# V of the second pass in seven products, and the scaling of head outputs one step later

## The chip, the cores and the metric

The kernel runs on one core of a Trainium2 chip. The metric is the device time of one execution in microseconds (us). Four engines do the work: TensorE (PE) multiplies, VectorE (DVE) and ScalarE (ACT) work elementwise, GpSimd (POOL) does some small operations; SyncE (SP) issues all transfers, on one queue.

## What is computed

One layer over 2048 tokens of width 1024. The core of the reference:

```python
h = rms_norm(x, g_pre[l]) * (1.0 + scale) + shift
(pv, pg, hq, hf, hi, hg, mg_pool, mg_hgrn) = jnp.split(h @ w_in[l], split_idx, axis=-1)
...
v = hi.astype(jnp.float32).reshape(shp)
o = hgrn2(q, k, v, logf)
o = rms_norm(o, hgrn_norm_g[l]).astype(x.dtype).reshape(b, s, HGRN_WIDTH)
branch_b = (o * jax.nn.silu(hg)) @ w_hgrn_o[l]
merged = jax.nn.sigmoid(mg_pool) * branch_a + jax.nn.sigmoid(mg_hgrn) * branch_b
y = merged @ w_out[l]
x = x + gate * rms_norm(y, g_post[l])
```

`hgrn2` is a gated linear recurrence over 8 heads of width 128, taken in chunks; branch A is a mixer of running means. V is `hi`: h times 1024 columns of `w_in`.

## The kernel before

The tokens go through in two passes of 1024, each as two halves `t` of 512 tokens. Numbers are split into a high and a low float32r part (`split`, L171: ACT casts the high part, DVE subtracts for the low part), and each product is taken as three matmuls (high x high, high x low, low x high), all with 512 columns moving.

A pass has these stages. **V** (`v_job`, L760): tokens on the stationary side, so V comes out with tokens on partitions; for each half `t`, each 512 columns `grp` and each k of 8 there are 4 token tiles x 3 matmuls, into four banks of the pool `pj`. ACT copies the four tiles (L787) and they are stored to DRAM (`Vd`), from where each head loads its part (`v_head`). **Heads** (loop at L1040): for each head three `quad`s (L469): fq (f and q), m (the two merge gates), gp (pool part and gate). A quad computes a 2 x 2 block product with the two token halves as columns, in seven products of 4 x 3 matmuls each instead of eight (Winograd's form of Strassen's scheme). The seven forms of h it needs (B11, B21, B22, T1 to T4) stay in SBUF in high and low parts: 7 x 4 x 2 = 56 of the 76 shared tiles of 128 x 512 (`up`, `utile`). **a_job, b_job**: the two branch projections. **y_job**: the last product, the norm and the residual.

The forms of h come from `h_in` (L436: four transposes on PE, then ACT, then the split) and `h_mix` (L456: four DVE differences, then four splits; "mix" below). In the second pass h of the second half and the four mixes are made during V: `x_cols` and `h_in` after each `v_job`, the mixes during the jobs of `t == 1` (L1026 to L1037).

Inside the head loop the recurrence of each head runs as two generators `hgrn` (L522, one per token half), of which every `tick()` (L961) does one step. There are six ticks in a quad and three more per head, 21 in all. The step of interest is near the end of `hgrn`, L679 to L698, and falls into the m quad of the next head (in head 7: its gp quad): after the output matmuls `po`, ACT sums squares (`junk`, L687), POOL takes the power -0.5 (`ss`, L688 and L689), ACT scales `on` (L692), and three steps later PE transposes it (`pot`, L698). In `quad`, the copy of bank `a` into bank `d` (L496: `pdfq`, `pdm`, `pdgp`) comes after the product T3, and product T4 is accumulated onto it.

Weights: `take()` (L266) gives the next item and prepares up to LOOK = 4 items ahead. In the first pass an item is loaded raw (`raw_load`, L174, buffers `wr`), combined and split into `whl` (buffers `whl`, four), and items that come again are stored to DRAM scratch (`keep`, L187); in the second pass they are loaded from there (`again`, L192). The order of the work on each engine follows the order in the code, except that an instruction whose inputs are late may be put behind others when the program is built.

Of the kernel before, what the change touches and what calls it, by code (L numbers as in the profile page):

```python
# [33 lines left out]
MASK_W = P + 2 * 64 + 5 * NT * 64  # L34
NU = 76
GAP = 5
KINDS = (("m", "gp"), ("gp", "m"))


# [30 lines left out]
def tile_block(ctx: ExitStack, tc: tile.TileContext, x, c, w_ada, b_ada, g_pre, g_post, w_in,  # L70
# [20 lines left out]
    def utile(name, dt=F32):  # L91
        return up.tile([P, T], dt, tag="u", name=name)
# [115 lines left out]
    def quad_items(key, oa, ob, keep_it):  # L208
# [37 lines left out]
            return [f0, f1, f2, f3, lambda: one(4, "21"), lambda: one(5, "12"), lambda: one(6, "22")]  # L246
        items.append((7, make))

    early = {}
    pending = []  # L250

# [41 lines left out]


    psa = [ph.tile([P, T], F32, tag=f"ph{i}", name=f"psa{i}") for i in range(2)]
    shv = cst.tile([P, 8], F32, name="shv")
    scv = cst.tile([P, 8], F32, name="scv")

# [223 lines left out]
    def hgrn(p, h, t, cx):  # L522
# [270 lines left out]
        cx["V"][h] = vt  # L793


    def two_out(nm, p, i, t, src, cx, stay):
# [42 lines left out]
    def b_job(p, j, cx):  # L839
        ps = [bank(f"psB{p}_{j}_{t}") for t in range(2)]  # L840
        sm = sig_in(p, j, 1, cx)
        for half in range(2):
            w = take()
            for t in range(2):
                three(ps[t], w, [cx["gG"][4 * half + i, t] for i in range(4)], half == 0, half == 1)
        for t in range(2):
            a, b = cx["a"].pop((j, t)), sm[t]
            tt(b, ps[t], b)
            tt(a, a, b, op=ADD)
            hi, lo = utile(f"mgh{p}_{j}_{t}", F32R), utile(f"mgl{p}_{j}_{t}", F32R)  # L850
            split(a, hi, lo)
            cx["mg"][j, t] = (hi, lo)
# [9 lines left out]
    def y_job(p, t, nn, q, cx):  # L862
# [36 lines left out]
        for tk in range(NT):  # L899
# [5 lines left out]
            for n2 in (0, 1):  # L905
# [9 lines left out]
                else:  # L915
                    outs.append(o)


    cxs = []
    for p in range(NPASS):  # L920
        cx = {k: {} for k in ("sm", "F", "Q", "G", "V", "pw", "Gd", "Pd", "Sd", "gP", "gG", "a", "mg", "x", "xc", "h32",
                              "mv", "y", "yss")}
        cx["Vd"] = dram(f"Vd{p}", [P, 8, D])
        for h in range(NH):
            cx["Gd"][h] = dram(f"Gd{p}_{h}", [P, 2, 2, T])
        for g in range(NG):
            cx["Pd"][g] = dram(f"Pd{p}_{g}", [P, 2, 2, T])
        for j in range(KT):
            for w in range(2):
                cx["Sd"][j, w] = dram(f"Sd{p}_{j}_{w}", [P, 2, T])  # L930
        cxs.append(cx)

    def krow(src, k, o):
        return src[k * P:(k + 1) * P, o:o + T]

    for p in range(NPASS):
# [17 lines left out]
        for t in range(2):  # L954
# [50 lines left out]
    for p in range(NPASS):  # L1005
        cx = cxs[p]

        mixes = [lambda p=p, i=i, cx=cx: h_mix(p, i, cx) for i in range(4)]
        if p == 0:
            head_in(0)  # L1010
            for q in range(4):
                hook = None
                if q < 3:
                    hook = lambda q=q: head_in(q + 1)
                if q == 3:
                    xss = [x_rows(NT + tk, SP.dma_start) for tk in range(NT)]
# [6 lines left out]
        vj = [(t, grp, q) for t in range(2) for grp in range(2) for q in range(4)]  # L1023
# [12 lines left out]
        while mixes:  # L1036
            once(mixes)  # L1037

        v_head(p, 0, cx)
        for h in range(NH):  # L1040
            if h + 1 < NH:
                v_head(p, h + 1, cx)
            n = f"{p}_{h}"

            def fq(row, t, u):
                (f_got, q_got)[row](p, h, t, u, cx)

            def gp(row, t, u):
                if row == 1:
                    g_got(p, h, t, u, cx)  # L1050
                elif h % 2 == 1:
                    pg_got(p, h // 2, t, u, cx)
                else:
                    gen = pv_got(p, h // 2, t, u, cx)
                    next(gen)
                    active.append(gen)

            steps = []

            def tick_in():  # L1060
                tick()
                once(steps)

            quad("fq" + n, cx, fq, tick)
            active.extend(hgrn(p, h, t, cx) for t in range(2))
            tick()
            for i, kind in enumerate(KINDS[h == NH - 1]):
                if kind == "gp":
                    quad("gp" + n, cx, gp, tick)
# [5 lines left out]
                tick()  # L1075
            if p + 1 < NPASS:
                x_stats(8 + h)

        for j in range(KT):
# [22 lines left out]
        for t in range(2):  # L1102
# [32 lines left out]
```

## Time and profile before

| | us |
|---|---|
| median of 3 runs | 1851.86 (1851.43 to 1857.75) |
| profiled execution | 1851.48 |
| its span, first to last instruction | 1849.7 |
| TensorE busy in the span | 1782.6 (96%) |
| VectorE / ScalarE busy | 1089.1 / 799.9 |

The span is what the profile shows; some 1.8 us of the execution lie around it. Matmuls are pipelined, so a busy TensorE is not at its peak, and the ends of matmuls are modelled. An engine's idle time counts only where it makes TensorE wait.

### The profile page before, as it was taken

To read this page: it belongs to the slowest core of one execution; us is meant where nothing else is said; L and a number is where in the kernel's file an instruction comes from. 1 tells how busy PE (TensorE), PEld (TensorE's weight loads), DVE (VectorE), ACT (ScalarE), POOL (GpSimd) and SP (SyncE) were. 2 spreads that over 40 slices of the span, in tenths; PEclk is the share of its full clock that TensorE was granted. 3 is DMA by queue.
4 is the path that set the end of the run, shared out by engine and by line. 5 is a ranking of instruction groups with operands and counts; after the bars stand their busy time and mean duration, and the time that the engine had idled before them with its cause. 6 is when DMAs were issued, how large, how long until landed. Compare 5 with 4: busy or idle time off the path is not lost.

```text
span 1849.7 us, 31713 instructions
## 1 busy us (share of the span) xinstructions
PE 1782.6 (96%) x12053; PEld 1456.7 (79%) x12053; DVE 1089.1 (59%) x2328; ACT 799.9 (43%) x1863; POOL 80.0 (4%) x136
## 2 busy tenths in 40 slices
PE   5999999999999999999999999999999999999997
PEld 4788878878888777787788778878888788788886
DVE  7568877887888884565432255465455456533322
ACT  4746656656556562223322335445344344311111
POOL 1100000000000000000000000000000000000000
PEclk9999999999999999999999999999999999999999
DMA  8697676676767759987887765664764764694476
GB/s 298 233 322 277 221 268 243 231 261 225 266 241 246 247 201 320 361 288 255 295 310 242 246 193 175 224 206 154 234 205 159 231 201 162 233 340 163 141 258 230
DMA packets 236530, 444.19 MB, mean 240 GB/s; under 512 B 18989, under 2 KB 109786, under 8 KB 236378
## 3 DMA queue, kind: packets, MB, share of 16 engines
q1 hardware_dynamic: 236378, 442.17, 69.9%
q8 instruction: 95, 1.56, 0.3%
q14 instruction: 57, 0.47, 0.1%
HBM read 269.61 MB, written 172.49 MB: 239 GB/s over the span
## 4 chain that ended last, share of the span: by engine, by line
PE 79%; ACT 6%; DMA 3%; DVE 3%; POOL 2%; issue 2%; SPq 1%; POOLq 0%; DVEq 0%; ACTq 0%
PE psB L278 9%; PE psV L278 8%; PE psy L278 8%; PE pafq L278 6%; PE pagp L278 6%; PE pam L278 5%; PE pefq L278 5%; PE psA L278 4%; PE pegp L278 4%; PE pem L278 3%; PE psa L278 3%; PE pbfq L278 2%; PE pbm L278 2%; PE pdfq L278 2%; PE pdm L278 2%; PE pbgp L278 2%
## 5 line engine op out<-in xcount | busy, mean ns | idle before, releaser
L172 DVE TENSOR_TENSOR whl<-wr,whl 128x512 fp32r<-128x512 f32 x210 | 143.7, 689 | 83.6 <-ACT whl L172 82.6
L172 ACT CAST whl<-wr 128x512 fp32r<-128x512 f32 x210 | 129.8, 620 | 128.6 <-DMA wr<-in_w_hgrn_o_dram 22.4
L278 PE MATMUL psy<-whl,mgh 128*128 128x512 f32 x512 | 160.1, 393 | 1.4 <-DVE y L390 0.7
L278 PE MATMUL psV<-whl,hB 128*128 128x512 f32 x512 | 161.3, 397 | 0.1
L278 PE MATMUL psB<-Gh,whl 128*128 128x512 f32 x512 | 158.6, 390 | 0.0
L578 DVE COPY_PREDICATED PT<-mask,psa 128x256 f32<-128x256 uint8 x160 | 86.1, 548 | 51.5 <-PE psa L278 51.5
L278 PEld LDWEIGHTS psy<-whl,mgh 128*128 128x128 f32 x512 | 95.0, 188 | 22.5 <-DMA whl<-scr_y 1.7
L278 PEld LDWEIGHTS psB<-Gh,whl 128*128 128x128 f32 x512 | 96.1, 188 | 20.5 <-issue 0.5
L278 PEld LDWEIGHTS psV<-whl,hB 128*128 128x128 f32 x512 | 96.6, 191 | 19.8 <-ACT V L787 0.3
L278 PE MATMUL psV<-whl,lB 128*128 128x512 f32 x256 | 100.8, 395 | 0.0
L278 PE MATMUL psB<-Gl,whl 128*128 128x512 f32 x256 | 100.0, 391 | 0.0
L278 PE MATMUL psy<-whl,mgl 128*128 128x512 f32 x256 | 100.0, 391 | 0.0
L278 PE MATMUL pam<-hT,whl 128*128 128x512 f32 x256 | 87.2, 402 | 0.0
L278 PE MATMUL pagp<-hT,whl 128*128 128x512 f32 x256 | 86.1, 397 | 0.0
L278 PE MATMUL psA<-Ph,whl 128*128 128x512 f32 x256 | 82.6, 397 | 3.4 <-DVE sm L390 1.7
L278 PE MATMUL pafq<-hT,whl 128*128 128x512 f32 x256 | 84.0, 389 | 0.0
L390 DVE TENSOR_TENSOR K<-K,TT 128x256 f32<-128x256 f32 x192 | 81.2, 424 | 1.0 <-PE psa L278 0.9
L278 PEld LDWEIGHTS psa<-X,K 128*32 128x32 f32 x2816 | 50.1, 110 | 29.8 <-issue 21.1
L172 ACT CAST mgh<-sm 128x512 fp32r<-128x512 f32 x32 | 19.7, 620 | 121.3 <-DVE sm L390 121.3
L390 DVE TENSOR_TENSOR y<-psy,gg 128x512 f32<-128x512 f32 x32 | 21.9, 688 | 73.9 <-ACT jy L893 73.7
L278 PE MATMUL psa<-X,K 128*32 128x48 f32 (+2 forms) x2816 | 61.0, 208 | 2.1 <-DVE PT L572 2.1
L572 DVE COPY_PREDICATED PT<-mask,psa 128x256 f32<-128x256 uint8 (+1 forms) x96 | 51.9, 541 | 18.3 <-PE psa L278 18.3
(358 smaller groups left out, 4307.5 us busy)
## 6 DMA issues: line engine op xcount, KB each, us to landing
wr<-in_w_in_dram SPq DMA_DIRECT2D x122, 256.0 KB, 4.4
whl<-scr_y SPq DMA_DIRECT2D x48, 512.0 KB, 4.4
sm<-Sd SPq DMA_DIRECT2D x64, 256.0 KB, 4.3
whl<-scr_v SPq DMA_DIRECT2D x32, 512.0 KB, 3.4
wa<-in_w_ada_dram SPq DMA_DIRECT2D x32, 256.0 KB, 5.4
x<-in_x_dram SPq DMA_DIRECT2D x32, 256.0 KB, 5.5
Vd<-V SPq DMA_DIRECT2D x32, 256.0 KB, 2.4
scr_v<-whl SPq DMA_DIRECT2D x16, 512.0 KB, 2.8
```

Source lines behind the costliest of these rows:

```text
L172: return A.copy(hi, src32), V.tensor_tensor(lo, src32, hi.bitcast(F32), op=SUB)
L278: PE.matmul(o, lhsT=l, rhs=r, start=start, stop=stop, skip_group_check=True)
L390: return (e or V).tensor_tensor(o, a, b, op=op)
L572: V.copy_predicated(dst.rearrange("p (c a) b -> p c a b", c=NT), m.unsqueeze(1).broadcast_to(shp), src.unsqueeze(2).broadcast_to(shp))
L578: V.copy_predicated(dst.rearrange("p (c q) a b -> p c q a b", c=NT), m, src.rearrange("p c (a b) -> p c a b", b=b).unsqueeze(2) .broadcast ...
```

## The change

Two switches are added, `FAST_V, FAST_Y = True, False`; what `FAST_Y` guards (the same form for y) is not executed, and is left out below.

1. In `hgrn`, one of the three `yield`s after the scaling moves ahead of it, so that `on` is issued one tick later; `pot` stays in its tick.
2. V of the second pass is taken by `rows7`, in seven products over both token halves and both column halves at once. The tokens' forms B11, B21, T1, T2, T3, B22, T4 are the stationary side; the moving side are seven combinations ("factors") of V's weights, 4 items each. B11, T2, T3, T4 accumulate in the four banks of `pj`, the products B21, T1 and B22 go to four other banks (`side`: the two of the scores and the two of `px`).
3. The factors are made in the first pass by `row_factors`, in 56 steps taken at every second tick of the head loop, in half widths of 256 columns, and stored to DRAM; the first pass's V weights are not stored any more.
4. The calls of `h_in` and the mixes that lay beside V are issued from `v_step`: h during B11, the mixes during B21.
5. The two score banks get new tiles at the head loop of each pass.

```diff
+    def row_factors(key, src):
+        steps = []
+        W = T // 2
+        for i in range(4):
+            for c0 in (0, W):
+                r = {}
+                def put(f, nm, i=i, c0=c0, r=r):
+                    w = utile(f"rf{key}{f}{i}{c0}", F32R)
+                    hi, lo = w[:, 0:W], w[:, W:T]
+                    split(r[nm], hi, lo)
...
+                    store((key, f, i), scr[key, f, i].rearrange("p (z n) -> p z n", z=2)[:, :, c0:c0 + W],
+                          w.bitcast(F32).rearrange("p (z n) -> p z n", z=2))
+                def ld(i=i, c0=c0, r=r):
+                    a, b = utile(f"ra{key}{i}{c0}"), utile(f"rb{key}{i}{c0}")
+                    for w, k in ((a, 2 * i), (b, 2 * i + 1)):
+                        SP.dma_start(...)
...
+                steps += [ld, nop, lambda two=two: two((0, "11"), (1, "12")),
+                          lambda two=two, a=sums: two(a, (2, "s1")),
+                          lambda two=two, a=sums2: two(a, (3, "11")),
+                          lambda two=two, a=sums3: two((4, "21"), a),
+                          lambda two=two: two((5, "12"), (6, "22"))]
+        return steps
...
         tt(ss, ss, mh[:, 0:NT], op=ALU.pow, e=G)
+        yield
         on = utile("on" + n)
         for cc in range(NT):
             A.activation(on[:, cc * P:(cc + 1) * P], po[:, cc, :], AF.Copy, scale=ss[:, cc:cc + 1])
-        yield
         yield
         yield
...
+    def rows7(name, mv, got, step):
+        acc = [bank(f"ra{name}{tk}") for tk in range(NT)]
+        c, s, u = ([utile(f"r{z}{name}{tk}") for tk in range(NT)] for z in "csu")
+        def done(nm, tk, ps):
+            if nm == "B11":
+                A.copy(c[tk], ps)
+            elif nm == "B21":
+                tt(c[tk], ps, c[tk], op=ADD)
+                got(0, 0, tk, c[tk])
+            elif nm == "T1":
+                A.copy(s[tk], ps)
...
+            else:
+                got(1, 0, tk, ps)
+        for nm in ("B11", "B21", "T1", "T2", "T3", "B22", "T4"):
+            ps = acc
+            if nm in ("B21", "T1", "B22"):
+                ps = [side(f"rx{name}{nm}{tk}", tk) for tk in range(NT)]
...
+            for i in range(2):
+                w = take()
+                for tk in range(NT):
+                    mul(i, w, tk)
+                step(nm, i)
+            ws = [take(), take(LOOK - 1)]
+            for tk in range(NT):
+                for i in (2, 3):
+                    mul(i, ws[i - 2], tk)
+                done(nm, tk, ps[tk])
+            step(nm, 2)
...
     for p in range(NPASS):
-        for t in range(2):
+        if p > 0 and FAST_V:
+            factor_items("v7")
+        for t in range(0 if p > 0 and FAST_V else 2):
             for grp in range(2):
                 for k in range(KT):
-                    plain_item(("v", grp, k), krow(w_in, k, O_I + grp * T), None, t == 1)
+                    plain_item(("v", grp, k), krow(w_in, k, O_I + grp * T), None, t == 1 and not FAST_V)
...
+            def v_step(nm, i):
+                if nm == "B11":
+                    for _ in range(len(late) if i == 2 else 2):
+                        once(late)
+                elif nm == "B21":
+                    for _ in range(2 if i == 2 else 1):
+                        once(mixes)
+            rows7(f"V{p}", cx["mv"], v_got, v_step)
...
+        psa[:] = [ph.tile([P, T], F32, tag=f"ph{i}", name=f"psa{p}_{i}") for i in range(2)]
+        behind_heads = []
+        if p == 0 and FAST_V:
+            behind_heads += row_factors("v7", w_in[:, O_I:O_I + D])
...
+        def htick():
+            tick()
+            every[0] += 1
+            if every[0] % 2 == 0:
+                once(behind_heads)
```

In the head loop `htick` takes the place of `tick`.

## Rows read from the trace of the kernel before

**Rows 1.** The page, part 1: busy us (share of the span) and instructions.

```profile
PE 1782.6 (96%) x12053; PEld 1456.7 (79%) x12053; DVE 1089.1 (59%) x2328; ACT 799.9 (43%) x1863; POOL 80.0 (4%) x136
```

**Rows 2.** Waits of PE: line, waited for; us in total, times, longest.

```profile
PE pdm L278 <- ACT pdm L496: 14.4, 12, 1.3
...
PE pdgp L278 <- ACT pdgp L496: 3.2, 2, 2.1
```

**Rows 3.** Timeline of ACT in head 1, first pass: start, us, line, operation.

```profile
234.06 1.14 ACT L692 ACTIVATE on<-po,ss 128x128 f32<-128x128 f32 x4 [1.41 <-POOL ss L390]
235.07 0.29 ACT L687 ACTIVATE junk<-po 128x128 bf16<-128x128 f32 x1
...
238.20 1.14 ACT L692 ACTIVATE on<-po,ss 128x128 f32<-128x128 f32 x4 [1.62 <-POOL ss L390]
239.22 0.61 ACT L496 COPY pdm<-pam 128x512 f32<-128x512 f32 x1
```

**Rows 4.** Timeline of POOL, the same head: the power of the second token half.

```profile
236.98 1.19 POOL L390 TENSOR_TENSOR ss<-ss,mh 128x4 f32<-128x4 f32 x1
```

**Rows 5.** Timeline of PE, the same head, from product T3 of m to gp.

```profile
235.54 0.39 PE L278 MATMUL pam<-hT,whl 128*128 128x512 f32 x1
...
238.26 0.39 PE L278 MATMUL pem<-hB,whl 128*128 128x512 f32 x1
239.89 0.50 PE L278 MATMUL pdm<-hT,whl 128*128 128x512 f32 x1 [1.24 <-ACT pdm L496]
...
242.75 1.04 PE L698 MATMUL pot<-ident,on 128*128 128x128 f32 x8
...
246.66 0.50 PE L278 MATMUL pegp<-hT,whl 128*128 128x512 f32 x1
```

**Rows 6.** Chain that ended last, through the second pass's V: start, us, what.

```profile
949.70 5.50 PE psV L278 x24
...
972.51 0.44 PE xT L444 x4
972.94 65.34 PE psV L278 x288
```

**Rows 7.** Timeline of DVE: one weight's low part, then the second pass's V.

```profile
240.48 0.68 DVE L172 TENSOR_TENSOR whl<-wr67s,whl 128x512 fp32r<-128x512 f32 x1
...
952.31 4.06 DVE L911 SCALAR_TENSOR_TENSOR xr<-y,yss,xr 128x512 f32<-128x512 f32 x6 [0.51 <-POOL yss L390]
...
974.50 0.69 DVE L172 TENSOR_TENSOR lB<-h,hB 128x512 fp32r<-128x512 f32 x1 [5.29 <-ACT hB L172]
975.11 0.68 DVE L390 TENSOR_TENSOR t<-h,h 128x512 f32<-128x512 f32 x1
...
998.36 0.69 DVE L390 TENSOR_TENSOR t<-h,h 128x512 f32<-128x512 f32 x1
...
1003.60 0.68 DVE L390 TENSOR_TENSOR t<-h,h 128x512 f32<-128x512 f32 x1
```

**Rows 8.** Timeline of PE early in the run.

```profile
39.47 1.05 PE L332 MATMUL psa<-one,acc 128*128 128x1 f32 x8 [1.37 <-DVE acc L325]
...
42.01 0.63 PE L278 MATMUL psV<-whl,hB 128*128 128x512 f32 x1
42.43 0.63 PE L278 MATMUL psV<-whl,lB 128*128 128x512 f32 x1
```

**Rows 9.** Busy us by stretch: PE, PEld, DVE, ACT, POOL, PEclk, DMA share, GB/s.

```profile
40.00:45.00 5.00, 5.00 (x20) 4.00 (x19) 4.01 (x10) 3.38 (x6) 0.00 (x0) 0.66 0.46 136
...
80.00:132.00 52.00, 52.00 (x235) 43.18 (x234) 34.89 (x56) 29.33 (x51) 0.00 (x0) 1.00 0.90 315
...
203.00:276.00 73.00, 70.78 (x575) 58.06 (x574) 58.55 (x129) 43.51 (x106) 3.89 (x6) 1.00 0.72 249
```

**Rows 10.** Groups by line and shape: a DVE operation on 128x256; busy, mean ns.

```profile
L390 DVE TENSOR_TENSOR K<-K,TT 128x256 f32<-128x256 f32 x192 | 81.2, 424 | 1.0 <-PE psa L278 0.9
```

**Rows 11.** DMA issues: transfers, KB each, median us to landing.

```profile
wr<-in_w_in_dram SPq DMA_DIRECT2D x122, 256.0 KB, 4.4
```

More of the change, by code (lines that the diff above doesn't have):

```diff
@@ L295, in tile_block, with side @@
     psa = [ph.tile([P, T], F32, tag=f"ph{i}", name=f"psa{i}") for i in range(2)]
+    def side(name, i):
+        if i < 2:
+            return ph.tile([P, T], F32, tag=f"ph{i}", name=name)
+        return px.tile([P, T], F32, tag="px", name=name)
     shv = cst.tile([P, 8], F32, name="shv")
@@ L793, in v_head, with mul @@
         cx["V"][h] = vt
+    def rows7(name, mv, got, step):
[9 more added lines that the diff above has]
+                A.copy(s[tk], ps)
+            elif nm == "T2":
+                tt(u[tk], ps, s[tk], op=ADD)
+            elif nm == "T3":
+                tt(s[tk], ps, s[tk], op=ADD)
+                got(1, 1, tk, s[tk])
+            elif nm == "B22":
+                tt(u[tk], ps, u[tk], op=ADD)
+                got(0, 1, tk, u[tk])
+            else:
[4 more added lines that the diff above has]
+                ps = [side(f"rx{name}{nm}{tk}", tk) for tk in range(NT)]
+            def mul(i, w, tk):
+                xh, xl = (z[:, tk * P:(tk + 1) * P] for z in mv[nm, i])
+                mm(ps[tk], xh, w[0], i == 0 and nm in ("B11", "B21", "T1", "B22"), False)
+                mm(ps[tk], xh, w[1], False, False)
+                mm(ps[tk], xl, w[0], False, i == 3)
+            for i in range(2):
[9 more added lines that the diff above has]
+            step(nm, 2)
     def two_out(nm, p, i, t, src, cx, stay):
@@ L849, in b_job @@
             tt(a, a, b, op=ADD)
+            if p == NPASS - 1 and FAST_Y:
+                cx["m32"][t, j] = a
+                if t == 0:
+                    part(p, ("B11", "B21")[j % 2] + "m", j // 2, a, cx)
+                elif j % 2 == 1:
+                    b11, b21, b12, b22 = (cx["m32"][z] for z in ((0, j - 1), (0, j), (1, j - 1), (1, j)))
+                    i = j // 2
+                    t1, t2 = utile(f"mt1_{i}"), utile(f"mt2_{i}")
+                    tt(t1, b12, b11, op=SUB)
+                    tt(b12, b22, b12, op=SUB)
+                    tt(t2, b22, t1, op=SUB)
+                    tt(b21, b21, t2, op=SUB)
+                    cx["m32"] = {**cx["m32"], ("T1", i): t1, ("T2", i): t2, ("T3", i): b12, ("B22", i): b22, ("T4", i): b21}
+                    for z in ((0, j - 1), (0, j), (1, j - 1), (1, j)):
+                        del cx["m32"][z]
+                continue
             hi, lo = utile(f"mgh{p}_{j}_{t}", F32R), utile(f"mgl{p}_{j}_{t}", F32R)
@@ L916, in y_job, with y_fast, x_in, got @@
                     outs.append(o)
+    def y_fast(p, cx):
+        rs = [[sp.tile([P, 2], F32, tag="ys7", name=f"ys7_{t}_{tk}", bufs=8) for tk in range(NT)] for t in range(2)]
+        ys, xr = {}, {}
+        def x_in(t, tk):
+            tok = p * 8 + t * NT + tk
+            for n in range(2):
+                xr[t, tk, n] = utile(f"xr{p}_{t}_{tk}_{n}")
+                gated(xr[t, tk, n], x[tok * P:(tok + 1) * P, n * T:(n + 1) * T])
+        def got(n, t, tk, src):
+            jy = sp.tile([P, T], BF16, tag="jx", name=f"jy{p}_{t}_{n}_{tk}", bufs=1)
+            A.activation(jy, src, AF.Square, scale=1.0 / 32, accum_out=rs[t][tk][:, n:n + 1])
+            y = utile(f"y{p}_{t}_{n}_{tk}") if (n, t) == (1, 0) else src
+            tt(y, src, cx["gg"][n])
+            ys[t, tk, n] = y
+            if n != 1 - t:
+                return
+            r = rs[t][tk][:, 0:1]
+            V.tensor_scalar(r, r, rs[t][tk][:, 1:2], EPS, op0=ADD, op1=ADD)
+            tt(r, r, mh[:, 0:1], op=ALU.pow, e=G)
+            tok = p * 8 + t * NT + tk
+            for n2 in range(2):
+                y, xx = ys.pop((t, tk, n2)), xr[t, tk, n2]
+                if n2 == 0 and t == 0 and tk == NT - 1:
+                    A.activation(y, y, AF.Copy, scale=r)
+                    tt(xx, y, xx, op=ADD, e=G)
+                else:
+                    V.scalar_tensor_tensor(xx, y, r, xx, op0=MUL, op1=ADD)
+                o = (out[tok * P:(tok + 1) * P, n2 * T:(n2 + 1) * T], xx)
+                if t == 1:
+                    outs.append(o)
+                else:
+                    while outs:
+                        store("out", *outs.pop(0))
+                    SP.dma_start(*o)
+        mv = {(k[0][:-1], k[1]): v for k, v in cx["mv"].items() if k[0][-1] == "m"}
+        nxt = {"B11": "T1", "B21": "T2", "T1": "T3", "T2": "B22", "T3": "T4"}
+        def step(nm, i):
+            if nm in nxt:
+                for k in ((0,), (1,), (2, 3))[i]:
+                    z = nxt[nm]
+                    part(p, z + "m", k, cx["m32"].pop((z, k)), cx)
+                    mv[z, k] = cx["mv"][z + "m", k]
+            if nm in ("T2", "T3"):
+                t = 1 if nm == "T2" else 0
+                for tk in ((0,), (1,), (2, 3))[i]:
+                    x_in(t, tk)
+        rows7(f"y{p}", mv, got, step)
@@ L919, in tile_block @@
     cxs = []
     for p in range(NPASS):
[L921 removed]
+        cx = {k: {} for k in ("sm", "F", "Q", "G", "V", "pw", "Gd", "Pd", "Sd", "gP", "gG", "a", "mg", "x", "xc", "h32", "m32",
                               "mv", "y", "yss")}
@@ L934, in krow, with factor_items @@
         return src[k * P:(k + 1) * P, o:o + T]
+    def factor_items(key):
+        for f in range(7):
+            for i in range(4):
+                items.append((1, lambda f=f, i=i: [again((key, f, i), f"{len(ready)}")]))
     for p in range(NPASS):
-        for t in range(2):
+        if p > 0 and FAST_V:
+            factor_items("v7")
+        for t in range(0 if p > 0 and FAST_V else 2):
             for grp in range(2):
                 for k in range(KT):
-                    plain_item(("v", grp, k), krow(w_in, k, O_I + grp * T), None, t == 1)
+                    plain_item(("v", grp, k), krow(w_in, k, O_I + grp * T), None, t == 1 and not FAST_V)
         for h in range(NH):
@@ L953, in tile_block @@
                            w_hgrn_o[half * T:(half + 1) * T, j * P:(j + 1) * P].rearrange(ko, p=P), P, p == 0)
-        for t in range(2):
+        if p == NPASS - 1 and FAST_Y:
+            factor_items("y7")
+        for t in range(0 if p == NPASS - 1 and FAST_Y else 2):
             for nn in range(2):
@@ L1022, in tile_block, with v_got @@
             late = [lambda k=k: h_in(0, 1, k, cxs[0]) for k in range(KT)]
-        vj = [(t, grp, q) for t in range(2) for grp in range(2) for q in range(4)]
+        if p > 0 and FAST_V:
+            def v_got(n, t, tk, src):
+                vt = src
+                if (n, t) == (1, 0):
+                    vt = utile(f"V{p}_{t}_{n}_{tk}")
+                    A.copy(vt, src)
+                store("Vd", cx["Vd"][:, t * NT + tk, n * T:(n + 1) * T], vt)
+            def v_step(nm, i):
[6 more added lines that the diff above has]
+            rows7(f"V{p}", cx["mv"], v_got, v_step)
+        vj = [] if p > 0 and FAST_V else [(t, grp, q) for t in range(2) for grp in range(2) for q in range(4)]
         if p == 0:
@@ L1074, in tile_block @@
                     quad("m" + n, cx, lambda row, t, u: m_got(p, h, row, t, u, cx), tick_in)
-                tick()
+                htick()
             if p + 1 < NPASS:
                 x_stats(8 + h)
+        while behind_heads:
+            once(behind_heads)
         for j in range(KT):
@@ L1101, in tile_block @@
                         steps.append(lambda p=p, t=t, k=k, nx=nx: h_in(p + 1, t, k, nx))
-        for t in range(2):
+        if p == NPASS - 1 and FAST_Y:
+            y_fast(p, cx)
+        for t in range(0 if p == NPASS - 1 and FAST_Y else 2):
             for nn in range(2):
```

29 lines of the change are left out of this document (25 added, 4 removed).

## The prediction

> **What bounds the kernel.** I read the page's busy shares first, then the waits of TensorE, then the timelines of four engines around the longest repeated wait, then the chain of waits through the second pass's V, and the stretches last. TensorE (PE) is busy 96% [rows 1], so only two things shorten the run: fewer matmuls, or waits of TensorE that go. The reader is to see in the waits of TensorE that one is periodic: `pdm` behind the ScalarE (ACT) copy of L496, 12 times, and its twin `pdgp` twice [rows 2]. That is 14 waits, one for each of heads 1 to 7 in both passes (head 7 runs gp before m, hence the other name).
>
> **Edit 1, the scaling one step on.** The timelines of one head [rows 3 to 5] show how the wait arises. ACT sums the squares of head h-1's outputs, POOL (GpSimd) raises them to -0.5 (1.19 us), and ACT stands in its queue for POOL before the four `on` copies: 1.41 us for the first half of the tokens, 1.62 us for the second. The remaining three squares of the second half stand behind the first half's `on` (235.07), so both POOL trips are in series with ACT. Only then comes the copy to `pdm` (239.22), although its source, the last `pam` matmul, began at 235.54 and takes 0.39 us. TensorE reaches the point at 238.26 + 0.23 = 238.49 and starts at 239.89: 1.40 us lost. The row of the wait says 1.24 because the modelled end (0.39) is longer than the step (0.23).
>
> With `on` one tick later the copy, ready at 235.93, is emitted ahead of it. Either it runs at once and ends near 236.6, or ACT still takes both `on` groups first: then the three squares move up by the wait and the `on` ahead of them, 235.07 - 1.41 - 1.14 = 232.5, POOL takes its second pair right behind the first (which ends as `on` starts, 234.06) and ends it near 234.1 + 0.3 + 1.2 = 235.6, the second `on` ends near 236.7 and the copy near 237.3. Both are over 1 us ahead of 238.49. What is late next would be `pot`, the transpose of `on`, at 242.75 [rows 5], then 1.40 us earlier, 241.35. If the copy and the sigmoid of the sum go first, eight `on` (2.3 us) end by about 240.5: 0.8 us to spare. No instruction is added. So the edit takes out 14.4 + 3.2 = 17.6 us of waits plus 14 x (0.39 - 0.227) = 2.3: **-19.9 us**. The ends: 10 us if the wait only moves to `pot` in part, 19.9 at best.
>
> **Edit 2, V of the second pass in seven products.** The stage has 2 x 2 x 8 x 4 x 3 = 384 matmuls of 512 columns; the seven products have 7 x 4 x 4 x 3 = 336. The chain shows 288 of them in 65.34 us, 0.227 each [rows 6]: 48 fewer are **-10.9 us**. The change leaves the matmul's shape and its loads of 128 x 128 as they are, so the step stays.
>
> It shortens a cover, though. The mixes of h (t1 and the T factors, four calls, 8 VectorE (DVE) operations each) had the 44 us of the second token half to hide under. The starts of two successive mixes on DVE are 998.36 and 1003.60 [rows 7]: 5.24 us each, 21 for four. Now they are issued during product B21 (10.9 us), and product T1 needs all four. Step by step, from V's start at 949.70 [rows 6]: TensorE does B11 with three groups of transposes (0.44 each) until 961.9, B21 until 972.8, and after 27 matmuls of T1, at 978.9, it needs the fourth mix. DVE: the epilogue of the first pass's y ends at 952.31 + 4.06 = 956.4 [rows 7]; two low parts and four scalings of x follow, about 2.8, to 959.2 (I assume x's loads have landed, since they no longer stand behind four output stores); the transposes of the last two h run to 960.1, and from the start of the last group to the end of its low part takes 972.51 to 975.19, 2.7 us [rows 6, 7], so 962.3. Three mixes to 978.0; of the fourth the sixth operation, 6 x 0.68 later [rows 7], 982.1; the four sums of B21 that come before it in the code, 0.68 each, make it 984.8. TensorE waits 984.8 - 978.9 = **+5.9 us**, whether in one piece or partly for the sums that free its banks. Bounds: 0 if DVE takes the mixes up earlier; 984 - 972.8 = 11.2 if all four mixes go ahead of the sums. I take the code's order.
>
> A gap has a second price. Early in the run TensorE did transposes and 128x1 products with waits between them (39.47), and behind that the matmuls step 42.01 to 42.43, 0.42 us, with a granted clock of 0.66 over the 5 us: the 1.2 GHz level in part of it [rows 8, 9]. Some ten matmuls at 0.2 us extra are **+2 us** (0 to 2; I take it, since a wait of 5.9 is longer than the 1.37 there). Sum of the edit: -10.9 + 5.9 + 2.0 = **-3.0**, between -10.9 and +2.3. The sums and copies of the later products (about 0.7 us each on DVE or ACT) lie beside 10.9 us of matmuls each. The loads fall from 32 of 512 KB to 28 at the same pace of one for 12 matmuls.
>
> **Edit 3, the factors made in the first pass.** Eight half-width sets, each 7 casts on ACT and 7 low parts and 4 sums on DVE of 128x256. The nearest row is 0.424 us [rows 10]: 88 on DVE are 37 us, 56 on ACT about 24 (an estimate at the same duration). They go out at every second tick, 21 ticks a head, so 56 steps fill 5.3 heads: 7 us of DVE a head. In one head DVE is busy 58.55 of 73 us [rows 9], so 14.5 are idle and half of them remain. The new work also needs tiles: 56 of the 76 shared ones hold h in seven forms, and a set takes four or five of the other 20. On SP's queue 16 loads and 56 stores come in and 16 stores go; a store waits for its low part on DVE, and behind it stand the raw weight loads, which land in 4.4 us [rows 11]. What hides all this is the lead of the weights: the low part at 240.48 belongs to the product that begins at 246.66, 6.2 us later [rows 5, 7]. A step puts at most 4 x 0.424 = 1.7 us into DVE's queue, well under that lead. Bounds 0 and +37; I take **+3**, near the lower end that the lead speaks for.
>
> The new banks for the scores (`psa`) in each pass add no work: nothing uses them when they are made.
>
> **The sum.** -19.9 - 3.0 + 3 = -19.9. The profiled execution took 1851.48 us (span 1849.7, 1.8 around it), 0.4 us under the median of 1851.86, so 1851.5 - 19.9 = **1832 us** (1831.6), 1.1% faster.
>
> **Rivals.**
> *DVE keeps ahead.* The mixes need only h of four tiles that are ready early, and DVE has idle stretches before 975. Then edit 2 gives its 10.9 in full: 1851.5 - 19.9 - 10.9 + 3 = 1824. Against it: in the old run the first mix (975.11) came right behind the last h's low part (974.50), with idle time before [rows 7]. Chance 0.15.
> *The sums are queued behind the mixes.* The T1 wait is then 11.2 plus the clock: edit 2 costs 2.3, 1837. For it: the sums wait for TensorE, and mixes could be put ahead of them. 0.11.
> *The wait moves to `pot`.* If ACT is late by more than the 0.8 us to spare, each head pays part of its 1.40 again. At half: 1851.5 - 10 - 3.0 + 3 = 1841. 0.10.
> *Slower: the first pass becomes bound by DVE.* In heads 0 to 5 of the first pass, from the point where DVE falls behind by more than the 6.2 us of lead (or the shared tiles run out and the sets block head work), each us of the sets lands on the path: 37 in place of 3, 1851.5 - 22.9 + 37 = 1866. Against it the 14.5 us idle per head. 0.06.
> *Slower: short runs choke the transfers.* The sets move runs of 1 KB, 72 transfers more. If raw loads land in three times 4.4 us, each quad's first factor is 8.8 - 6.2 = 2.6 late; 16 quads make 42 us: 1832 + 42 = 1874. Against it: from 80 to 132 us the engines were 0.90 busy and TensorE lost nothing, and the heads stand at 0.72 [rows 9]. 0.02. The Trainium skill, "Perfetto Trace Analysis", section "DMA Optimizations", says that transfers under 2 KB have significant overhead each; by that rule alone this rival would weigh more, and no row before shows such stores.
>
> **The numbers.** The forecast case (1826 to 1840 by its own terms) has 0.56. A measurement of this kernel tells about 0.5%, 9.3 us, from no change. Faster by more than that: the forecast case nearly whole, 0.53, the first two rivals 0.24, half the `pot` case 0.05: 0.82. Slower: the last two, a little under 0.08: 0.07. The rest 0.11. The range 1822 to 1845 leaves out the end of the first rival and the two slow ones.
>
> **What would show it.** No wait of TensorE for L496 in either pass, and no new one for `on`. 336 matmuls between the end of y and the second pass's first head, with one wait of 3 to 8 us in or ahead of T1, put down to the T1 factor's low part or the sums on DVE, and then a clock below 1.00 for some us. DVE about 7 us busier in heads 0 to 5 of the first pass, TensorE without waits for weights there. I am wrong if the `pdm` waits stay, if the V stage takes 88 us or more, or if the first pass's heads get longer.

## The result, and the profile after

The changed kernel takes **1841.1 us** (median of 6 runs, 1835.4 to 1847.3), the kernel before 1853.4 us (median of 6, 1851.4 to 1857.8): a ratio of 0.9932 with a 95% interval of 0.9909 to 0.9955. It is 12.3 us faster, where 1832 us was predicted against a range of 1822 to 1845. The sign and the range hold; of the 19.9 us forecast, 12.3 came.

The profiled execution took 1843.7 us, its span is 1841.9 us. The starts of the first matmul of each stage on TensorE's timeline cut the spans of the two kernels into stretches (us), and the same cuts serve for the main runs below ("copy first" is the run with `on` held behind the copy):

| stretch | before | after | edit 1 alone | edit 1 undone | copy first | copy first, V as before |
|---|---|---|---|---|---|---|
| start to head 0 | 130.9 | 133.7 | 130.4 | 130.7 | 130.8 | 132.5 |
| heads, first pass | 572.1 | 570.2 | 565.8 | 581.8 | 557.8 | 557.7 |
| projections and y, first pass | 246.5 | 244.2 | 245.3 | 246.4 | 243.4 | 246.1 |
| V, second pass | 88.7 | 84.6 | 88.7 | 85.9 | 83.2 | 88.7 |
| heads, second pass | 570.3 | 567.3 | 566.4 | 570.6 | 559.9 | 559.2 |
| rest | 241.2 | 241.9 | 242.9 | 241.2 | 240.8 | 241.5 |
| span | 1849.7 | 1841.9 | 1839.5 | 1856.6 | 1815.9 | 1825.7 |

The second and third columns say where to look. V became 4.1 us shorter, and the heads, where 17.6 us of waits were to vanish, only 1.9 and 3.0. Each column is one execution. (The first stretch, from which the change only takes the stores of V's weights, is 2.8 us longer; the granted clock over the first 130 us was 0.97 in this execution and 0.99 in that of before.)

The page's busy times, beside [rows 1]:

```profile
PE 1776.9 (96%) x12005; PEld 1451.2 (79%) x12005; DVE 1126.8 (61%) x2432; ACT 814.6 (44%) x1915; POOL 79.1 (4%) x136
```

The 48 matmuls are gone, and DVE and ACT have the factors' work. The waits of TensorE, beside [rows 2]:

```profile
PE pdm L325 <- ACT pdm L549: 12.2, 12, 1.9
```

The reader is to see that the wait the change was to remove is still there, 12 times of 12. Its twin `pdgp` is gone. One of the longer ones, in head 1 of the first pass, on TensorE:

```profile
237.92 0.39 PE L325 MATMUL pam<-hT,whl 128*128 128x512 f32 x1
...
240.64 0.39 PE L325 MATMUL pem<-hB,whl 128*128 128x512 f32 x1
242.89 0.50 PE L325 MATMUL pdm<-hT,whl 128*128 128x512 f32 x1 [1.86 <-ACT pdm L549]
```

and on ACT:

```profile
236.91 0.37 ACT L746 ACTIVATE on<-po,ss 128x128 f32<-128x128 f32 x1 [0.98 <-POOL ss L443]
237.17 0.27 ACT L740 ACTIVATE junk<-po 128x128 bf16<-128x128 f32 x1
...
237.42 0.37 ACT L746 ACTIVATE on<-po,ss 128x128 f32<-128x128 f32 x1
237.67 0.29 ACT L740 ACTIVATE junk<-po 128x128 bf16<-128x128 f32 x1
...
238.17 0.30 ACT L740 ACTIVATE junk<-po 128x128 bf16<-128x128 f32 x1
...
241.21 1.14 ACT L746 ACTIVATE on<-po,ss 128x128 f32<-128x128 f32 x4 [2.09 <-POOL ss L443]
242.22 0.61 ACT L549 COPY pdm<-pam 128x512 f32<-128x512 f32 x1
```

The copy's source is ready at 237.92 + 0.39 = 238.31. It starts at 242.22, because the second `on` group stands ahead of it and that group waits 2.09 us for POOL with ACT idle. The code now issues `on` behind the copy, and ACT runs it ahead all the same. Moreover the last three squares (`junk`) of the second half did not move up: first `on` group and squares alternate one by one, so POOL gets its second set only at 238.66. The Trainium skill, "PSUM — Partial Sum Buffer", section "Engine vs sequencer instructions", calls ACT's queue strictly first in, first out; these rows agree, as 2.09 us of idle time passed with a ready copy in line behind the four waiting `on`.

In V of the second pass, the waits of TensorE from 948.3 to 1032.9:

```profile
PE xT L497 <- DVE xc L485: 2.4, 1, 2.4
PE raV L325 <- DMA whl<-scr_v: 1.7, 1, 1.7
PE rxV1T L325 <- ACT hT L173: 1.0, 1, 1.0
PE rxV1B L325 <- DMA whl<-scr_v: 0.3, 1, 0.3
```

T1's wait for its factor is the third row, 1.0 us instead of the 5.9 forecast. The larger ones are for the last columns of x and for a weight.

### The profile page after: what moved, and what is told of

The parts are those of the page before. It is cut to its first block, busy times and chain, and to the rows that moved or that the text cites. A ratio compares the mean times of both kernels' runs of the same rounds, so it can differ in the third digit from the quotient of the medians.

```text
span 1841.9 us, 32010 instructions
## 1 busy us (share of the span) xinstructions
PE 1776.9 (96%) x12005; PEld 1451.2 (79%) x12005; DVE 1126.8 (61%) x2432; ACT 814.6 (44%) x1915; POOL 79.1 (4%) x136
## 4 chain that ended last, share of the span: by engine, by line
PE 76%; ACT 6%; DVE 5%; DMA 4%; POOL 2%; issue 2%; SPq 1%; POOLq 0%; DVEq 0%; ACTq 0%
PE psB L325 9%; PE psy L325 8%; PE pagp L325 6%; PE pafq L325 6%; PE pefq L325 4%; PE pam L325 4%; PE pegp L325 4%; PE psA L325 4%; PE psV L325 3%; PE psa L325 3%; PE pem L325 2%; PE pbfq L325 2%; PE pdm L325 2%; PE raV L325 2%; PE pdfq L325 2%; PE pbgp L325 2%
## 5 line engine op out<-in xcount | busy, mean ns | idle before, releaser
L325 PE MATMUL psV<-whl,hB 128*128 128x512 f32 x256 | 83.5, 409 | 1.4 <-ACT V L840 1.4
L443 DVE TENSOR_TENSOR sm<-psB,sm 128x512 f32<-128x512 f32 x32 | 22.1, 690 | 63.3 <-PE psB L325 61.8
L1010 ACT ACTIVATE jy<-psy 128x512 bf16<-128x512 f32 x32 | 19.1, 597 | 92.1 <-PE psy L325 91.1
```

What stands on the lines that cost most here:

```text
L325: PE.matmul(o, lhsT=l, rhs=r, start=start, stop=stop, skip_group_check=True)
L443: return (e or V).tensor_tensor(o, a, b, op=op)
L1010: A.activation(jy, pss[tk], AF.Square, scale=1.0 / 32, accum_out=rs[:, nn:nn + 1])
```

## Experiments

Theory: in the heads it is the order of instructions on ACT that decides, and the gain missing there is the copy to `pdm` still standing behind `on`. Rivals: the factors' added work keeps the copy late; edit 1 gave its 19.9 us and something else took half back; the V stage is bound by the mixes on DVE.

**1. Edit 1 undone.**

```diff
-        yield
         on = utile("on" + n)
...
         yield
         yield
+        yield
```

> The changed kernel with only edit 1 undone: the scaling `on` is issued in the same step as the squares again. Theory (order on ACT): the later step did little, because ACT takes both `on` groups ahead of the copy to `pdm` in either form; edit 1 is worth only the difference of the waits in the two profiles, 14.4 + 3.2 before against 12.2 after, 5.4 us, so 1841 + 5 = 1846 us, with `pdm` waits of about 1.2 us each and the two `pdgp` waits back. Rival (edit 1 gave its 19.9 us, and something else took half of it back): 1841 + 20 = 1861 us.

Measured 1855.4 us, ratio 1.0004 (0.9990 to 1.0018). So edits 2 and 3 alone gave nothing that the runs can tell, and edit 1 is worth some 14 us in the changed kernel, between the two expectations. The waits show why it is more than 5: they did not stay at 17.6, they are 19.4 + 3.2 = 22.6 us.

```profile
PE pdm L325 <- ACT pdm L549: 19.4, 12, 3.3
...
PE pdgp L325 <- ACT pdgp L549: 3.2, 2, 2.2
```

In the old order the factors make those of the first pass longer (12.7 us of `pdm` against 7.7 before; in the second pass both have 6.8). Head 2 of the first pass, ACT and then DVE:

```profile
310.58 1.15 ACT L745 ACTIVATE on<-po,ss 128x128 f32<-128x128 f32 x4 [1.70 <-POOL ss L443]
311.60 0.42 ACT L173 CAST rfv<-rav 128x256 fp32r<-128x256 f32 x1
311.90 0.61 ACT L549 COPY pdm<-pam 128x512 f32<-128x512 f32 x1
```
```profile
312.06 0.43 DVE L173 TENSOR_TENSOR rfv<-rav,rfv 128x256 fp32r<-128x256 f32 x1 [2.65 <-ACT rfv L173]
```

A factor's cast stands in the same queue ahead of the copy (0.3 us from its start to the copy's), and DVE waits behind that cast. The heads of the first pass are 581.8 us long, 9.7 more than before.

**2. Edit 1 alone.**

```diff
-FAST_V, FAST_Y = True, False
+FAST_V, FAST_Y = False, False
```

> The kernel before with edit 1 alone: no row factors, V of the second pass as before. Theory (order on ACT): the `pdm` waits stay, about 0.8 us each in both passes as in the second pass of the changed kernel, 12 x 0.8 = 9.6, and `pdgp` is gone: 1853.4 - (17.6 - 9.6) = 1845 us. Rival (the extra work of the row factors on ACT and DVE keeps the copy late, not the order): without that work the waits vanish and edit 1 gives its 19.9 us, 1833 us.

Measured 1840.5 us, ratio 0.9923 (0.9907 to 0.9938): the whole gain of the change, from its smallest part. It lies between the expectations again, nearer the theory (4.5 us under it, 7.5 over the rival), and the waits decide for the theory: they shrink and stay.

```profile
PE pdm L325 <- ACT pdm L549: 7.8, 12, 0.9
```

**3. Factors made and not used.**

```diff
+MAKE_V, FAST_V, FAST_Y = True, False, False
...
-        if p == 0 and FAST_V:
+        if p == 0 and MAKE_V:
             behind_heads += row_factors("v7", w_in[:, O_I:O_I + D])
```

> Edit 1 and edit 3 without edit 2: the row factors are made and stored in the first pass and not used; V of the second pass is computed as before, from the stored V weights, so 16 stores of 512 KB are made that the changed kernel drops. Against the run with edit 1 alone it prices edit 3. Theory: the factors lengthen the odd heads of the first pass (waits of 1.6 to 1.9 us in place of 0.8, and matmuls at a lower granted clock behind them), about 3 x 1 us of waits and 3 us of clock: 4 to 8 us over the run with edit 1 alone. Rival (the lead of the weights covers them): within 1 us of it. In the third case, DVE and DMA both at their limit, 15 us or more.

Measured 1842.2 us, ratio 0.9939 (0.9925 to 0.9954), 1.7 us over run 2, which the runs' spread cannot tell from nothing. The profile can: the heads of the first pass take 569.3 us against 565.8, and the `pdm` waits are 12.7 us against 7.8. Edit 3 costs some 3.5 us there in this one execution, a little under the 4 expected.

**4. `on` held behind the copy.**

```diff
...
-        A.copy(d, a)
+        cpy[0] = A.copy(d, a)
...
         on = utile("on" + n)
-        for cc in range(NT):
-            A.activation(on[:, cc * P:(cc + 1) * P], ...)
+        with after(cpy[0]):
+            for cc in range(NT):
+                A.activation(on[:, cc * P:(cc + 1) * P], ...)
```

`after(x)` makes what is issued under it follow x in the queue of x's engine; it adds no wait between engines.

> The changed kernel with the eight `on` copies held behind the latest copy to `pdm` (or `pdgp`) in ACT's own queue; nothing else changes. Theory (order on ACT): the copy runs as soon as the last `pam` matmul ends, the 12 waits (12.2 us) go, and up to 14 x 0.16 us of steps with them: 1841 - 12 to 14 = 1827 to 1829 us, and `pot` does not wait. Rival 1 (the copy is late of its own, because of the added work): the waits stay, 1841 us. Rival 2 (the wait moves to `pot`, since `on` ends 1 us or more later): half of it comes back as waits of `pot`, 1835 us.

Measured **1821.1 us**, ratio 0.9825 (0.9805 to 0.9845), 20 us under the changed kernel. No `pdm` wait is left. Head 1 of the first pass, ACT and then TensorE:

```profile
235.41 0.57 ACT L551 COPY pdm<-pam 128x512 f32<-128x512 f32 x1 [1.18 <-PE pam L325]
235.90 1.40 ACT L749 ACTIVATE on<-po,ss 128x128 f32<-128x128 f32 x5
...
238.15 0.87 ACT L749 ACTIVATE on<-po,ss 128x128 f32<-128x128 f32 x3
```
```profile
237.71 0.39 PE L325 MATMUL pem<-hB,whl 128*128 128x512 f32 x1
237.93 0.39 PE L325 MATMUL pdm<-hT,whl 128*128 128x512 f32 x1
...
240.66 1.04 PE L754 MATMUL pot<-ident,on 128*128 128x128 f32 x8
```

The copy now waits for its source and not for POOL, `pdm` follows `pem` without a gap, and `on` ends at 239.02, 1.6 us ahead of `pot`. By the table the heads give 12.4 + 7.4 = 19.8 us. In the second pass the waits were 4.9 us, and 6 x 0.16 for the steps makes 5.8 of the 7.4. In the first pass the waits were 7.3 and the steps 1.0, and 3.4 us are clock (last section): 11.7 of the 12.4.

**5. Squares first, copy left free.**

```diff
...
-            A.activation(junk[:, 0:P], po[:, cc, :], AF.Square, ...)
+            sq[0] = A.activation(junk[:, 0:P], po[:, cc, :], AF.Square, ...)
...
+        with after(sq[0]):
...
```

> The changed kernel with the eight `on` copies held only behind the last square of the second half of the tokens; the copy to `pdm` is left free, and ACT now has the squares of both halves, then both `on` groups, then the copy. It is the second way in which the prediction had the wait go: POOL's two trips run one behind the other while ACT is still squaring. Theory (the alternation of squares and `on` puts POOL's second trip in series, and that alone makes the copy late): the waits shrink to 0.3 us or less, and the time comes near that of the run with the copy first, 1821 to 1825 us. Rival (the copy must stand ahead of `on`; behind both groups it is late whatever the squares do): 12 waits of about 1 us stay, 1835 to 1841 us.

Measured 1820.6 us, ratio 0.9822 (0.9798 to 0.9847): not to be told from run 4, and no `pdm` wait is listed. ACT in head 1 and then TensorE:

```profile
236.97 1.14 ACT L749 ACTIVATE on<-po,ss 128x128 f32<-128x128 f32 x4
238.49 1.14 ACT L749 ACTIVATE on<-po,ss 128x128 f32<-128x128 f32 x4 [0.39 <-POOL ss L443]
239.51 0.61 ACT L551 COPY pdm<-pam 128x512 f32<-128x512 f32 x1
```
```profile
240.21 0.39 PE L325 MATMUL pem<-hB,whl 128*128 128x512 f32 x1
240.44 0.39 PE L325 MATMUL pdm<-hT,whl 128*128 128x512 f32 x1
```

Both groups stand ahead of the copy, and it is in time. So it need not go first: what made it late was POOL's second trip in series with ACT, and the alternation of squares and `on` put it there. (In this execution V of the second pass took 87.9 us, with the code of run 4's 83.2; the last section shows why.)

**6. x for the second pass two steps earlier, on top of run 4.**

```diff
                     if t == 1:
                         once(late)
+                        if nn == 1 and q in (1, 2):
+                            once(late)
```

> The run with `on` held behind the copy, and in addition the last loads of x for the second pass (`x_cols` of the fourth column group) and one transpose group are issued two output steps earlier, in the last part of the first pass's y instead of in the V stage. Theory (the stage is held up by the order of the loads, not by DVE's mixes): the wait for `xc` of 1.6 to 2.4 us goes, and the mixes start earlier, so that part of the 1.0 us for `hT` goes too: 2 to 3 us under the run without it, 1818 to 1819 us. Rival (DVE, with the y epilogue, is what is late): x lands earlier and its scaling is no sooner, 1821 us.

Measured 1818.2 us, ratio 0.9809 (0.9789 to 0.9829). V shrinks from 83.2 to 79.0 us, where 336 x 0.227 plus two groups of transposes make 77.2. One wait is left at its border; it ends as V's first matmul starts, so the table's cuts count it to the stretch ahead:

```profile
PE raV L325 <- DVE y L443: 1.5, 1, 1.5
```

The waits for `xc` and `hT` inside V are gone, so the loads' place was the cause and DVE's mixes were not. The stretch ahead of it grew from 243.4 to 246.1 us: 1.5 of it is the wait above, some 0.4 the group of transposes that moved there, and the rest I do not place. So of the 4.2 us that V lost, the two stretches together kept 1.5. The total, 3 us lower, cannot be told from run 4's by 4 runs each.

**7. Copy first, V as before.** Run 4's edit with the switch of run 2.

> The kernel before with edit 1 and with `on` held behind the copy; no row factors, V of the second pass as before. It measures edit 1 at its full size, and, against the run with both, edits 2 and 3 where no wait in the heads mixes with them. Theory (the waits of before, 17.6 us, plus 14 x 0.16 us of steps, were the whole prize, as the prediction had it): 1853 - 20 = 1833 us, and edits 2 and 3 then gain 12 us on top of it (1833 - 1821). Rival (the waits also cost clock: stretches at the lower granted clock behind the longer of them go too): 1826 us or less, and edits 2 and 3 gain 5 us or less, as the length of the V stage says (4 us shorter).

Measured 1828.0 us, ratio 0.9863 (0.9848 to 0.9879). Edit 1 at its full size is worth 24.5 us (1852.5 - 1828.0), between the 20 of the theory and the 27 of the rival. The profiled execution of before had a granted clock of 1.00 from 203 to 640 us and this run's the same mean clock (0.997), and their spans differ by 24.0 us, so clock is not the surplus. Two more waits of before, the second in three heads of the first pass, are not in this run's list:

```profile
PE pot L698 <- ACT on L692: 2.2, 1, 2.2
PE psa L278 <- DVE PT L572: 2.1, 3, 1.0
```

With them 17.6 + 2.3 + 4.3 = 24.2. The sum comes near, but other waits differ between the two executions as well, so its last term is not shown. Against this run, run 4 prices edits 2 and 3 together: 6.9 us of gain, 5.5 of it in V, and the heads of the first pass as long with the factors (557.8) as without (557.7).

**8. y of the second pass in seven products too, on top of run 6.** The code that `FAST_Y` guards does for y what the change does for V.

```diff
-FAST_V, FAST_Y = True, False
+FAST_V, FAST_Y = True, True
```

> The run with the copy first and x earlier, with the switch for y of the second pass turned on as well: the last product is computed in seven products from stored factors of the output weights, which are made in the second pass's heads. 48 more matmuls of 0.227 us go, 10.9 us. Theory (V as measured: of 10.9 us some 4 remain in the stage, and the factors cost about 2 us in the heads): 2 to 6 us under the run without it, 1812 to 1816 us. Rival (the end of the kernel, where the sums on DVE and the output stores follow the last products with nothing beside them, grows by more than the matmuls save): 5 us or more over it, 1823 us or more.

Measured **1811.9 us**, ratio 0.9781 (0.9764 to 0.9798), 6.3 us under run 6, a little more than the 2 to 6 of the theory, and the fastest here. The last stage takes 89.6 us, against 98.5 in run 6, so 8.9 of the 10.9 stay; the heads of the second pass give back 1.2.

**9 and 10. What of the factors makes the copy later.** Two runs on top of run 3, one without the factors' DVE work (the sums go as well), one without their ACT casts.

```diff
...
-                    split(r[nm], hi, lo)
+                    A.copy(hi, r[nm])
...
```
```diff
...
-                    split(r[nm], hi, lo)
+                    V.tensor_tensor(lo, r[nm], r["11"], op=SUB)
...
```

> The run with the factors made and unused, less the factors' VectorE work: the 56 low parts and the 32 sums are left out (the high half is stored twice), while the 56 casts on ACT, the loads and the stores stay. In the run with them POOL's 128x4 operation on the sums of squares takes 1.44, 0.74, 1.45, 0.73 and 1.10 us for the second token half in heads 1 to 5 of the first pass, and 0.19 without the factors; each time it ends with a VectorE operation of two inputs. Theory (edit 3 costs through POOL, which VectorE's two-input operations hold up): the operation falls to 0.6 us or less, the `pdm` waits of heads 1, 3 and 5 of the first pass fall from 1.5 to 2.0 to 1 us or less, and the time is that of the run with edit 1 alone, 1840.5 us. Rival (the casts on ACT or the transfers are what makes the copy late): the waits stay at 1.5 to 2.0 us and the time at 1842 us.

> The counterpart: the factors' 56 casts on ACT are left out (the low half, taken as a difference of two raw blocks, is stored twice), while all 88 VectorE operations, the loads and the stores stay. Theory (VectorE holds POOL): POOL's operation stays at 0.7 to 1.4 us in heads 1 to 5 of the first pass and the `pdm` waits there at 1.2 us or more in at least three heads. Rival (ACT's casts): the waits fall to those of the run with edit 1 alone, 0.6 us in three heads and none in three.

Measured 1843.7 us (ratio 0.9954, 0.9936 to 0.9971) without the DVE work and 1841.6 us (0.9939, 0.9918 to 0.9961) without the casts. The waits, in this order:

```profile
PE pdm L323 <- ACT pdm L547: 13.3, 12, 2.0
```
```profile
PE pdm L325 <- ACT pdm L549: 13.4, 12, 2.2
```

Both runs keep the long waits (1.0 to 2.0 us in heads 1 to 5 without the DVE work, 1.2 to 2.2 without the casts), so neither the factors' VectorE work nor their casts alone is what makes the copy late: the theory of the first run falls and the rival of the second. The second run's theory holds as far as it went (POOL's operation took 0.5 to 1.4 us), but the first shows that POOL is held up without the factors' VectorE work too:

```profile
383.85 1.43 POOL L739 TENSOR_SCALAR ss<-ss 128x4 f32<-128x4 f32 x1 [1.78 <-ACT junk L738]
```

This is the second token half in head 3: it takes as long as with all of the factors' work, beside DVE operations that the kernel has anyway; in heads 1 and 2 it fell to 0.5 and 0.2 us. It looks as if either part of edit 3 shifts the head's instructions against each other, so that others of them meet POOL's. Which shift does it is open, and the transfers alone were not tried; run 4 shows that it costs nothing once the copy no longer waits for POOL.

## Why the prediction was right and where it was wrong

That 1841 lies in the range is in part luck: the waits that were to go stayed, and the range reached up to 1845 for other reasons.

**Edit 1 (-19.9 us forecast; 12.4 alone, 14 in the changed kernel, 24.5 with the order settled).** The waits, their number and their cause were read rightly: run 4 takes them away by the order on ACT and nothing else. The step that failed is the choice of only two orders: "either it runs at once", or "ACT still takes both `on` groups first: then the three squares move up by the wait and the `on` ahead of them". A third came, squares and `on` in turn. Run 5 shows that the second branch was sound as arithmetic: with the squares up, the copy behind both groups is in time. What I took for granted in it is that the squares of the second half, issued one step ahead of every `on`, are run ahead of them; on ACT's timeline three of them were not, and POOL's second trip stayed in series: 12.2 us of `pdm` waits in place of none. The size of the prize was too small as well: the two waits shown with run 7, for `pot` and for `psa`, went too. The first hangs on `on` itself; how the second does is not shown.

**Edit 2 (-3.0 forecast, -4.1 measured in the stage).** The net was near by luck of composition. The wait for T1's factor was put at 5.9 us and is 1.0. The mixes were not sooner than forecast (the operation put at 984.8 ended at 989.2); it was not one long wait because T2's matmuls were run between those of T1:

```profile
978.01 1.20 PE L325 MATMUL rxV1T<-whl,hT 128*128 128x512 f32 x4 [1.00 <-ACT hT L173]
...
982.75 0.74 PE L325 MATMUL raV<-whl,hT 128*128 128x512 f32 x2 [1.69 <-DMA whl<-scr_v]
...
984.73 0.62 PE L325 MATMUL rxV1T<-whl,hT 128*128 128x512 f32 x2
```

The 2.0 us of lower clock did not come in this execution: the stretch from 949 to 1040 ran at 1.00. (With the same code of V a lower clock did come in the executions of run 1, 0.83 from 990 to 1000 or 1.7 us, and of run 5, 3.4 us; see the last section.) In their place stand two terms I had at nothing. "I assume x's loads have landed" failed: the load was issued at 954.74, inside the stage, and DVE idled for it.

```profile
961.03 1.30 DVE L485 TENSOR_SCALAR xc<-xc,rst 128x256 f32<-128x256 f32 x4 [4.80 <-DMA xc<-in_x_dram]
```

And "the same pace of one for 12 matmuls" left no room for waits on weights, and there are 1.7 + 0.3 us of them. The weights' loads share SP's queue with the stores of V, which now wait for sums on DVE:

```profile
974.06 1.76 SPq L108 DMA_DIRECT2D Vd<-rcV  x2
975.91 1.46 SPq L195 DMA_DIRECT2D whl<-scr_v  x2
```

The first of these two loads stood behind a store that its sum released at 975.5. That this is what made T2's weight late is not shown: its own load, the second, went out at 977.0, when TensorE had just freed the buffer, and run 6 has the same order in the queue and no such wait.

Of the 10.9 us, 5.4 are these four waits and 4 x 0.16 their steps; some 0.8 more I do not place. A slip in the prediction's upper bound changes nothing: by its own steps the four mixes end at 962.3 + 21.0 = 983.3, not 984.

**Edit 3 (+3 forecast, +4.4 measured: 570.2 against 565.8 in the first pass's heads).** The size is near by luck, for its place was not foreseen. DVE is busier as forecast, 64.63 us from 203 to 276 against 58.55 [rows 9], and the lead of the weights covered it: no wait for a raw weight is listed in those heads. The cost came through edit 1's own wait, which grew to 1.9 us in heads 1 and 3 (0.4 with edit 1 alone), and through the clock behind it. The factors lengthened a chain on which TensorE already waited; costing the edit only by the cover of the weights missed that.

**The rivals.** "The wait moves to `pot`" gave 1841, which is the time measured, by another mechanism: `pot` never waits, the wait stayed where it was. DVE did not become the bound. The short runs did not choke the transfers; from the page after:

```profile
wr<-in_w_in_dram SPq DMA_DIRECT2D x122, 256.0 KB, 4.8
...
scr_v<-rfv SPq DMA_DIRECT2D x56, 256.0 KB, 3.5
```

The stores in runs of 1 KB land in 3.5 us, and the raw loads in 4.8 against 4.4 [rows 11]. By the rule of the Trainium skill ("Perfetto Trace Analysis", "DMA Optimizations") on transfers under 2 KB more was to be feared, if a run of 1 KB counts as one (each store is 256 KB); with the copy first, the first pass's heads are 0.1 us longer with these stores than without.

**What would have shown it** was named: "I am wrong if the `pdm` waits stay". They stayed.

## What to carry to other kernels

Moving a statement in the code moves it on its engine only if nothing puts it back: read the engine's own timeline, and where the order matters tie the instruction to the one that it must follow, as one line did here for 20 us. A wait of TensorE that hangs on a chain over two other engines can grow with what else those engines are given (here from 7.7 to 12.7 us in the first pass), so remove it before adding work; the same two edits that gave nothing beside the wait (run 1) gave 7 us without it (run 4 against run 7). When a stage is shortened, check which loads and stores stand in one queue inside it.

## What the hardware showed

**The clock behind a wait.** In the heads of before, 12 waits of 1.1 to 1.3 us left the granted clock at 1.00. In the changed kernel, behind the wait of 1.86 us at 242.89 (columns as in [rows 9]):

```profile
203.00:276.00 73.00, 71.14 (x572) 58.68 (x571) 64.63 (x150) 47.00 (x116) 4.63 (x6) 0.98 0.86 302
240.00:245.00 5.00, 3.14 (x11) 2.19 (x10) 2.15 (x6) 3.49 (x10) 1.09 (x2) 0.86 0.40 123
245.00:250.00 5.00, 5.00 (x23) 4.16 (x22) 4.16 (x9) 3.40 (x6) 0.00 (x0) 0.80 0.92 367
```

That is part of the time at 1.2 instead of 2.4 GHz and costs 5 x 0.14 + 5 x 0.20 = 1.7 us, nearly as much as the wait. Head 3 repeats it (349 to 422 also at 0.98), hence the 3.4 us of run 4's sum. A wait's length alone does not settle it. The 2.4 us wait in V had no such sequel (clock 1.00), and the wait for `pdgp` in head 7 of the first pass, 2.15 us long both before and with edit 1 undone, had none in the first and one in the second; before, then run 1:

```profile
677.00:682.00 5.00, 4.17 (x22) 3.57 (x23) 4.19 (x8) 3.71 (x10) 0.00 (x0) 1.00 0.40 131
```
```profile
685.00:690.00 5.00, 4.22 (x12) 3.32 (x13) 4.24 (x8) 3.66 (x8) 0.00 (x0) 0.66 0.42 136
```

In V too it is one execution and not another. Run 5 had waits of 2.3 and 1.8 us there, as the changed kernel had 2.4 and 1.7, and behind each the clock fell:

```profile
945.00:955.00 10.00, 7.74 (x32) 6.21 (x31) 2.07 (x6) 2.88 (x5) 0.00 (x0) 0.83 0.63 198
970.00:980.00 10.00, 8.18 (x29) 6.29 (x29) 9.65 (x15) 4.36 (x8) 0.00 (x0) 0.83 0.24 83
```

That is 2 x 10 x 0.17 = 3.4 us, and 87.9 - 3.4 = 84.5 is the changed kernel's 84.6. So the price that the prediction set behind a gap in V exists, and one profile does not tell whether a run pays it. The spread of the changed kernel's runs goes with the clock: 1835.4 us at a mean clock of 0.997, 1847.3 us at 0.992.

**POOL held by DVE.** POOL's operation on 128x4 elements takes 0.19 us in one head and 1.42 in another. The long one in head 1, and DVE beside it:

```profile
238.66 1.42 POOL L741 TENSOR_SCALAR ss<-ss 128x4 f32<-128x4 f32 x1 [1.78 <-ACT junk L740]
```
```profile
238.64 0.72 DVE L240 TENSOR_TENSOR wr<-wr67s,wr 128x512 f32<-128x512 f32 x1
239.28 0.40 DVE L443 TENSOR_TENSOR X<-sq,TT 128x256 f32<-128x256 f32 x1
239.61 0.41 DVE L443 TENSOR_TENSOR sq<-sq,TT 128x256 f32<-128x256 f32 x1
```

It ends at 240.08, just behind the third of three DVE operations that read two tiles of SBUF (240.02). With edit 1 alone (run 2), the same operation, from 235.21, fell beside a COPY_PREDICATED from 234.94, which reads one tile of SBUF and one of PSUM, and took 0.19. The Trainium skill, "SBUF — State Buffer", section "🎯 Summary: rules for kernel authors", says that of DVE with two SBUF inputs and a GpSimd operation that reads SBUF the second to issue is blocked until the first is done; the rows agree that POOL is held, and here it was held past the first operation to the end of the third. That is not so each time: the first half's operation in run 2 ended at 232.27, just behind one such DVE operation (232.22), although the next had followed without a gap:

```profile
231.74 0.53 POOL L741 TENSOR_SCALAR ss<-ss 128x4 f32<-128x4 f32 x1 [31.98 <-ACT junk L740]
```

What decides how many it is held by is not shown.
